# Mixer B of a two-layer hybrid encoder: when the k scaling, the weight units, the y loads and some evictions stand in the queues

## The chip, the cores and the metric

The kernel runs on one core of a Trainium2 chip. A core has five engines that run their own instruction queues in order: TensorE (PE: matmuls and transposes), VectorE (DVE), ScalarE (ACT), GpSimd (POOL) and SyncE (SP, which here only issues transfers). They meet through semaphores. Transfers run beside them. The metric is the device time of one execution in microseconds (us), the median of several runs, less is better.

## The reference

An encoder trunk of two layers over 1024 tokens of width 1024, in float32. Each layer is: RMS norm, one projection to q, k, v and a gate, attention, `(attention * silu(gate)) @ w_out`, residual; then an input embedding of 256 columns is projected, gated by a sigmoid of the normalised stream and added. Layer 0 attends over a neighbourhood (mixer A). Layer 1 (mixer B) is grouped-query attention, 16 query heads and 4 key/value heads of 64, cut to what matters here:

```python
proj = h @ w_in
q, k, v, gate = jnp.split(proj, [MIX_WIDTH, MIX_WIDTH + kv_w, MIX_WIDTH + 2 * kv_w], axis=-1)
q = rms_norm(q.reshape(b, s, B_Q_HEADS, HEAD_DIM), q_norm_g)   # per head
k = rms_norm(k.reshape(b, s, B_KV_HEADS, HEAD_DIM), k_norm_g)
q, k = _apply_axial_rope(q, tabs), _apply_axial_rope(k, tabs)
sc = einsum('bkgqd,bksd->bkgqs', q, k) / 8 ; pr = softmax(sc)
o = einsum('bkgqs,bksd->bkgqd', pr, v)
return (o * jax.nn.silu(gate)) @ w_out
```

## The kernel before

**Split operands.** Nearly every product is made from a high and a low half of each operand: `split3` issues three matmuls for one product. The stream h stands transposed in `HTh` and `HTl` (8 token tiles x 8 column blocks), weights come as units of 128 x 1024 numbers.

**Weight units.** The class `Weights` (object `WQ`) walks a fixed list of units. A unit goes through three steps: SP loads it into one of two `wstage` buffers, ACT copies it to its high half (line 235, `wh`, or `KA` where it takes such a slot), DVE subtracts to get the low half (line 240, `wl` or `KB`). Only after the subtraction is its `wstage` buffer free for the next load. `pump` does one step of this at each pulse: a unit is split when it is at least `age` pulses old, and a load is issued when at least `lag` pulses have gone by since the last split. Both are 3 in the stretch of the change. A pulse is the end of one item of the hand-written order (a piece of projection, a softmax, a block of transposes). At a pulse, actions that were put off by so many pulses (`post.add(n, f)`) also become due.

**Entry of mixer B** (about 725 to 775 us). Items in the order of `pre`: `first` (q, k, v of kv heads 0 and 1, two items to a token tile), the gate of pair 0 (`gates(0)`, two halves: matmuls `d<-HTh,KA` and `o<-HTh,KA`), then `second` (q, k, v of kv heads 2 and 3, one unit to an item, four items to a tile), with two key stacks `k_stack(0, hf)` between. `k_stack` transposes the scaled k tiles on PE (line 1277), ACT copies them (1280, 1285), POOL copies them across (1291, 1292). Each k tile is scaled by its norm in `finish_norm`: after 4 tiles DVE makes 1/sqrt in eleven small steps (lines 1206, 335 to 343), then ACT scales k (line 1236, eight 128 x 64 pieces) and POOL scales q. A gate half that is done is copied from PSUM by ACT (line 625, `G`), then goes through tanh (626). There is one PSUM buffer `d`: the next product in it waits for that copy.

**Attention steps** (from about 770 us). 128 steps n = (head, half, t). Step n puts, in this order of items: the transposes of n (`f_T`: 8 on PE into two `t` buffers, each copied by ACT to `PTh`, line 1397, and subtracted by DVE to `PTl`, line 1398), the exponentials of n + 1 (`f_E`, ACT, line 1383), the scores of n + 2 (`f_S`, PE, then DVE's minimum `mn`, line 1377), and at even n the products with V of the two steps before (`f_AV`). Projections fill the room between. A projection tile of `second` that ends there is evicted by ACT: copy to `th` (1314), square (1196), two copies to V (1320).

**The last steps.** From n = 111 or so the projection work is `pp_items`: the input embedding times its weight, copied by ACT to `th` (line 656) and stored by SP to `ppD` (line 657). `th` has two buffers, so such a copy waits until the store from two copies before has landed; the copy of a query stack (line 1349) takes a `th` buffer too. The attention result y of pairs 0 to 6 went to DRAM (`yD1h`, `yD1l`, SP, line 606) and comes back into `HTh`, `HTl` for the output projection: `load_y(1, t)`, line 290, two transfers of 448 KB for a tile. For token tiles 0 to 3 ACT's queue issues them, for 4 to 7 SP's; one tile to a step, tile t at n = 118 + t. Pair 7 stays on the chip: ACT writes its high half into `HTh` (`hi`, line 591), DVE its low half (`lo`, line 594), 3 and 5 pulses after the pair's first half is done.

The lines that the change touches, quoted where they act:

```python
                post.add(3, hi)
                post.add(5, lo)
...
                    for raw, rs in tiles:
                        post.add(2, lambda raw=raw, rs=rs: scale_tile(raw, rs, act if rs.shape[1] == 2 else pool))
...
                    if YLOAD_B <= n < YLOAD_B + NT:
                        att.append((lambda t=n - YLOAD_B: load_y(1, t), 0.0))
```

Of the kernel before, what the change touches and what calls it, by code (L numbers as in the profile page):

```python
# [15 lines left out]
AF = mybir.ActivationFunctionType  # L16
# [5 lines left out]
NT = 8  # L22
# [25 lines left out]
QO = (4, 6)  # L48
AGE, LAG = 3, 3
YS = (11, 11)  # L50
YLOAD_A, YLOAD_B = 0, 118
OPEN3 = 5
ULOAD = 5
TAGS_A = [("th", 512, 2), ("tb", 640, 2), None, ("G", 512, 3)]
# [109 lines left out]
def trunk(ctx, tc, x, wts, rpb, gains, hgains, mask, sides, rope, gain0, out):  # L164
# [196 lines left out]
    def pulse():  # L361
        WQ.pump()
        post.tick()
# [153 lines left out]
    def head_end(sb, h, hf, rs, Ops, ylive, layer, gg, talloc):  # L517
# [63 lines left out]
        def fin_last():  # L581
            dve.tensor_tensor(Y, Y, G, ALU.mult)
            if "rb" not in tail:
                post.l = [e for e in post.l if e[1] is not across]
                across()
            dve.tensor_tensor(Y, Y, tail["rb"], ALU.mult)
            y3 = Y.rearrange("p (t c) -> p t c", t=4)
            ts = slice(4 * hf, 4 * hf + 4)

            def hi():  # L590
                act.activation(HTh[:, ts, 7, :], y3, AF.Copy)

            def lo():
                dve.tensor_tensor(HTl[:, ts, 7, :], y3, HTh[:, ts, 7, :], ALU.subtract)
            if hf == 0:
                post.add(3, hi)
                post.add(5, lo)
            else:
                hi()
                lo()  # L600
# [533 lines left out]
    def mixer_b(pend):  # L1134
        with ExitStack() as es:
# [63 lines left out]
            def normed(t):  # L1199
                return range(t - 3, t + 1) if t % 4 == 3 else ()  # L1200

            def finish_norm(ss, tiles):
                wk = sb.tile([128, 96], F32, name="wk", bufs=1)
                n = ss.shape[1]
                if pro[0]:
                    ops = [lambda: dve.tensor_scalar(ss, ss, 0.5 / HD, 0.5 * EPS, op0=ALU.mult, op1=ALU.add)]
                    ops += rsqrt_ops(ss, ss, wk)
                    for i in range(2):
                        post.add(1 + i, lambda i=i: [f() for f in ops[6 * i:6 * i + 6]])
                    for raw, rs in tiles:  # L1210
                        post.add(2, lambda raw=raw, rs=rs: scale_tile(raw, rs, act if rs.shape[1] == 2 else pool))
                    return
                y, a = wk[:, 0:n], wk[:, n:2 * n]

                def power():
                    dve.tensor_scalar(ss, ss, 4.0 / HD, 4.0 * EPS, op0=ALU.mult, op1=ALU.add)
                    for c in range(0, n, 8):
                        w = slice(c, min(c + 8, n))
                        pool.tensor_tensor(y[:, w], ss[:, w], mhalf[:, :w.stop - c], ALU.pow)

                def newton():
                    dve.tensor_tensor(a, y, y, ALU.mult)
                    dve.scalar_tensor_tensor(a, a, -1.0, ss, op0=ALU.mult, op1=ALU.mult)
                    dve.scalar_tensor_tensor(ss, a, 3.0, y, op0=ALU.add, op1=ALU.mult)
                post.add(DR, power)
                at = DR + NP + (8 if n > 16 else 0)
                post.add(at - 1, newton)
                for i, (raw, rs) in enumerate(tiles):
                    post.add(at + i, lambda raw=raw, rs=rs: scale_tile(raw, rs))
# [67 lines left out]
            def qkv_items(i, eng, kstep):  # L1297
                keys = [("bqkv", i, u) for u in range(4)]
                items = []
                st = {}  # L1300
                for t in range(NT):
                    def evac(ps, t=t):
                        if t == 0:
                            KR[i] = qtp.tile([128, NT, 128], F32, name="qt")
                            for j in range(2):
                                V[2 * i + j] = vp.tile([128, NT, 128], F32R, name="V")
                            st["ss"] = sb.tile([128, NT, 6], F32, name="ss")
                        if t % 4 == 0:
                            QT[i, t // 4] = qtp.tile([128, 4, 256], F32, name="qt")
                        ss = st["ss"]  # L1310
                        tabq, tabk = st.pop("tab")
                        qt, kr = QT[i, t // 4][:, t % 4], KR[i][:, t]
                        raw = sb.tile([128, 512], F32, name="th")
                        act.activation(raw, ps, AF.Copy)
                        red = sumsq(raw[:, :384], 6, ss[:, t])
                        vs = []
                        for j in range(2):
                            v = V[2 * i + j][:, t]
                            c = raw[:, 384 + 64 * j:448 + 64 * j]
                            act.activation(v[:, :64], c, AF.Copy)  # L1320
                            vs.append((v, c))

                        def rot():
                            red()
                            rope_in(kr, raw[:, 256:384], tabk, eng)
                            rope_in(qt, raw[:, :256], tabq, eng)
                            for v, c in vs:
                                eng.tensor_tensor(v[:, 64:], c, v[:, :64], ALU.subtract)
                        post.add(1 if pro[0] else DR, rot)
                        us = normed(t)  # L1330
                        if us:
                            finish_norm(ss[:, us[0]:t + 1].rearrange("p t c -> p (t c)"),
                                        [(KR[i][:, u], ss[:, u, 4:6]) for u in us] +
                                        [(QT[i, u // 4][:, u % 4], ss[:, u, 0:4]) for u in us])

                    def alloc(t=t):
                        st["tab"] = load_tab(0, t), load_tab(1, t)
                        return dalloc()
                    items += proj_N(keys, t, 512, alloc, evac, release=keys if t == NT - 1 else (), kstep=kstep)
                return items  # L1340

# [80 lines left out]
            def gates(p):  # L1422
                return [i for hf in range(2) for i in gate_items("bg", p, hf, dalloc, sb, gg)]

            def stacks(i):
                return [(lambda hf=hf: k_stack(i, hf), 450.0) for hf in range(2)]
            first, second = qkv_items(0, dve, 4), qkv_items(1, pool, 2)
            ks, gf = stacks(0), gates(0)
            pre = first[:12] + ks[:1] + first[12:14] + [glue(lambda: q_stack(0, 0))] + first[14:]
            pre += gf + second[:2] + ks[1:] + second[2:6]  # L1430
# [2 lines left out]
            for i, d in enumerate(pre):  # L1433
                if pend and (i == 1 or i >= 2 and i % 2 == 0):
                    to_ht(psT, *pend.pop(0))
                if not pend:
                    WQ.hold = ("ple", 1, 0, 0)
                d[0]()
                pulse()
            pro[0] = False  # L1440

            def exps(n):
# [10 lines left out]
            for g in range(4):  # L1453
                att = []
                for n in range(32 * g, 32 * g + 32):
                    h, hf, t = steps[n]
                    av = n >= 2 and n % 2 == 0
                    w = CB if av else CN
                    def turn():
                        if WQ.gate:  # L1460
                            WQ.gate = False
                        later.tick()
                    att.append((turn, w[0]))
                    if av:
                        att.append((lambda n=n: f_AV(*steps[n - 1]), w[1]))
                    te = [(blocks(n), w[2])]
                    if n + 1 < len(steps):
                        te.append((exps(n + 1), w[3]))
                    if n % 2 == 0 and n > 0:
                        te.reverse()  # L1470
                    att += te
                    if n + 2 < len(steps):
                        def scores(n=n):
                            f_S(*steps[n + 2])
                            WQ.gate = n % 2 == 1 and n % 8 != 5 if n < 126 else None
                        att.append((scores, w[4]))
                    if n in (37, 41):
                        att.append((lambda n=n: turned.append(lambda: k_stack(1, n // 41)), 0.0))
                    m = n + QS_AT
                    if m % 8 == 0 and m < len(steps):  # L1480
                        hn, fn, _ = steps[m]
                        att.append((lambda hn=hn, fn=fn: turned.append(lambda: q_stack(hn // 2, fn)), 0.0))
                    if YLOAD_B <= n < YLOAD_B + NT:
                        att.append((lambda t=n - YLOAD_B: load_y(1, t), 0.0))
                if g == 3:
                    def last():
                        end[0] = 1
# [484 lines left out]
```

## Time and profile before

| | us |
|---|---|
| median of 3 runs | 1490.86 (1490.63 to 1491.48) |
| the profiled execution, its own time | 1492.02 |
| its span, first to last instruction | 1490.2 |
| around the span | 1.8 |
| PE busy in the span | 1470.3 (99%) |
| granted TensorE clock, mean | 0.999 |

In a timeline row stand the start and the length in us, the engine, the line, the operation, what it writes and reads, the sizes, how many instructions the row merges, and in brackets the engine's idle time before it with what ended it. The chain of waits is followed back from the last instruction: start, length, and what ran. A matmul's end is modelled, so matmuls overlap in the rows; two that follow each other without a wait start some 0.23 us apart, while each lasts 0.39.

### The profile page before, as it was taken

How to read it: one execution, taken by the hardware profiler on the slowest of the kernel's cores; microseconds unless marked ns; L12 is line 12 of the kernel's file. 1: busy time of each engine (PE TensorE's matmuls, PEld its weight loads, DVE VectorE, ACT ScalarE, POOL GpSimd, SP SyncE). 2: the span in 40 equal slices, each digit the busy share in tenths (PEclk: the TensorE clock that was granted, in tenths of full speed). 3: DMA queues.
4: the chain of work that ended last, by engine and by line, in shares of the span. 5: the costliest groups of instructions: out<-in, count | busy, mean ns of one | idle time of the engine just before them, and what ended most of it. 6: DMA issues, size and time to landing. Idle time of an engine off the chain costs nothing.

```text
span 1490.2 us, 23430 instructions
## 1 busy us (share of the span) xinstructions
PE 1470.3 (99%) x8305; PEld 1270.7 (85%) x8305; DVE 1053.9 (71%) x1915; ACT 914.6 (61%) x1836; POOL 464.8 (31%) x647
## 2 busy tenths in 40 slices
PE   8999999999999999999999999999999999999997
PEld 6888888988988887888878888999999988888886
DVE  5467776477477598657757687877878787689845
ACT  5477766477477635433456777777767777744532
POOL 2246775387265200020144342324141400000000
PEclk9999999999999999999999999999999999999999
DMA  8224564283122862262220111101102112763223
GB/s 262 99 89 159 103 164 138 65 170 100 36 89 85 326 254 99 92 204 86 68 78 12 40 50 45 42 17 50 51 28 64 37 64 73 246 234 109 78 95 128
DMA packets 91460, 157.61 MB, mean 106 GB/s; under 512 B 18256, under 2 KB 54352, under 8 KB 90832
## 3 DMA queue, kind: packets, MB, share of 16 engines
q1 hardware_dynamic: 87344, 143.80, 28.8%
q0 software_dynamic: 2560, 8.39, 3.8%
q10 hardware_dynamic: 1440, 3.94, 0.9%
q8 instruction: 66, 1.08, 0.3%
q14 instruction: 50, 0.41, 0.1%
HBM read 125.56 MB, written 50.83 MB: 118 GB/s over the span
## 4 chain that ended last, share of the span: by engine, by line
PE 55%; DVE 4%; ACT 2%; issue 1%; DMA 1%; POOL 0%; ACTq 0%; POOLq 0%; DVEq 0%
PE d L324 27%; PE s L324 10%; PE o L324 8%; PE t L1395 7%; PE t L506 1%; PE t L324 1%; PE t L1347 0%; DVE PTl L1398 0%; DMA HTl<-yD1l 0%; DVE xn L1749 0%; ACT wh L235 0%; DVE X L1638 0%; DVE wl L240 0%; DVE mn L1377 0%; DVE wl L1536 0%
## 5 line engine op out<-in xcount | busy, mean ns | idle before, releaser
L324 PE MATMUL d<-wh,HTh 128*128 128x512 f32 (+1 forms) x800 | 285.5, 358 | 2.0 <-ACT G L625 0.8
L324 PE MATMUL d<-wl,HTh 128*128 128x512 f32 (+1 forms) x800 | 281.7, 354 | 0.8 <-DVE wl L240 0.8
L324 PE MATMUL d<-wh,HTl 128*128 128x512 f32 (+1 forms) x800 | 282.5, 355 | 0.0
L1398 DVE TENSOR_TENSOR PTl<-t,PTh 128x512 fp32r<-128x512 f32 x256 | 164.7, 685 | 110.0 <-ACT PTh L1397 109.4
L324 PE MATMUL d<-HTh,wh 128*128 128x512 f32 x480 | 193.8, 404 | 0.0
L324 PE MATMUL d<-HTh,wl 128*128 128x512 f32 x480 | 188.7, 393 | 0.0
L324 PE MATMUL d<-HTl,wh 128*128 128x512 f32 x480 | 188.2, 392 | 0.0
L324 PEld LDWEIGHTS d<-wh,HTh 128*128 128x128 f32 x800 | 150.5, 189 | 24.8 <-ACT G L625 1.2
L324 PEld LDWEIGHTS d<-wl,HTh 128*128 128x128 f32 x800 | 150.8, 189 | 23.3 <-DVE wl L240 1.6
L324 PEld LDWEIGHTS d<-wh,HTl 128*128 128x128 f32 x800 | 150.8, 189 | 22.0 <-DVE wki L902 0.3
L1383 ACT ACTIVATE P<-s,mn 128x1024 f32<-128x1024 f32 x128 | 142.9, 1117 | 41.7 <-DVE mn L1377 40.6
L1397 ACT ACTIVATE PTh<-t 128x512 fp32r<-128x512 f32 x256 | 138.7, 594 | 42.1 <-PE t L1395 41.2
L1377 DVE TENSOR_REDUCE mn<-s 128x1 f32<-128x1024 f32 x128 | 154.8, 1210 | 5.1 <-PE s L324 4.7
L849 POOL TENSOR_TENSOR PTh<-PTh,SIDE 128x256 fp32r<-128x256 f32 x96 | 83.9, 874 | 168.2 <-ACT PTh L844 168.1
L1395 PE MATMUL t<-ident,P 128*128 128x128 f32 x1024 | 133.8, 273 | 1.3 <-DVE PTl L1398 1.3
L324 PE MATMUL s<-KA,QS 128*128 128x512 f32 (+2 forms) x384 | 134.8, 405 | 0.0
L1395 PEld LDWEIGHTS t<-ident,P 128*128 128x128 f32 x1024 | 116.6, 141 | 11.7 <-DVE PTl L1398 4.4
L324 PE MATMUL s<-KB,QS 128*128 128x512 f32 (+2 forms) x384 | 121.4, 370 | 0.0
L324 PE MATMUL o<-PTh,V 128*128 128x256 f32 (+2 forms) x672 | 118.6, 287 | 2.6 <-ACT PTh L1397 0.9
L324 PE MATMUL o<-PTl,V 128*128 128x256 f32 (+2 forms) x672 | 120.2, 290 | 0.5 <-DVE mn L821 0.5
L240 DVE TENSOR_TENSOR wl<-wstage,wh 128x1024 fp32r<-128x1024 f32 x76 | 95.0, 1252 | 34.6 <-ACT wh L235 34.5
L324 PEld LDWEIGHTS o<-PTh,V 128*128 128x128 f32 x672 | 98.6, 190 | 11.4 <-ACT PTh L1397 4.1
(286 smaller groups left out, 2930.0 us busy)
## 6 DMA issues: line engine op xcount, KB each, us to landing
wstage<-in_wts SPq DMA_DIRECT2D x88, 512.0 KB
pp<-ppD SPq DMA_DIRECT2D x32, 256.0 KB
X<-in_x SPq DMA_DIRECT2D x15, 512.0 KB
rb<-rD SPq DMA_DIRECT2D x58, 128.0 KB
ppD<-th SPq DMA_DIRECT2D x20, 256.0 KB
tD0t<-in_wts SPq DMA_DIRECT2D x16, 256.0 KB
tD1t<-in_wts SPq DMA_DIRECT2D x16, 256.0 KB
xD<-X SPq DMA_DIRECT2D x8, 512.0 KB
```

The costliest lines, as they stand in the source:

```text
L240: eng.tensor_tensor(lo[:, c:c + n], s[:, c:c + n], hi[:, c:c + n], ALU.subtract)
L324: pe.matmul(ps, a, b, start=first, stop=last, skip_group_check=True)
L506: pe.transpose(ps[:, k], xn[:, (4 * c + k) * 128:(4 * c + k + 1) * 128], ident)
L849: pool.tensor_tensor(pt[:, 3 * j - 1:3 * j + 4:4], pt[:, f1:f1 + 1].to_broadcast([128, 2, 128]), SIDE[:, :2], ALU.mult)
L1377: dve.tensor_reduce(mn, ps, axis=AX.X, op=ALU.min)
L1383: act.activation(p, ps, AF.Exp, bias=mn, scale=-1.0, accum_out=RS[h, hf][:, t:t + 1])
L1395: pe.transpose(ps[:, i], p[:, k * 128:(k + 1) * 128], ident)
L1397: act.activation(PTh[:, ks, c], ps, AF.Copy)
L1398: dve.tensor_tensor(PTl[:, ks, c], ps, PTh[:, ks, c], ALU.subtract)
```

## The change

It has five parts.

1. `KS_LATE = 5`: in the entry, the ACT scaling of k for tiles 4 to 7 is due 5 pulses after their last tile's eviction, and no longer 2. The scaling of q on POOL and of tiles 0 to 3 stays.
2. From item 14 of `pre` to its end, `WQ.age, WQ.lag` are 2, 1 where they were 3, 3.
3. `YLOAD_B = (114, 118)`: y tiles 0 to 3 are loaded at n = 114 to 117 where it was 118 to 121. Tiles 4 to 7 stay at n = 122 to 125.
4. The square and the two copies to V of an eviction of `second` are put off by one pulse once the entry is over.
5. The low half of pair 7's first half is due after 10 pulses where it was 5.

```diff
-YLOAD_A, YLOAD_B = 0, 118
+YLOAD_A, YLOAD_B = 0, (114, 118)
+KS_LATE = 5
...
-                post.add(5, lo)
+                post.add(10, lo)
...
-            def finish_norm(ss, tiles):
+            def finish_norm(ss, tiles, late=2):
...
-                        post.add(2, lambda raw=raw, rs=rs: scale_tile(raw, rs, act if rs.shape[1] == 2 else pool))
+                        key = rs.shape[1] == 2
+                        post.add(late if key else 2, lambda raw=raw, rs=rs, key=key: scale_tile(raw, rs, act if key else pool))
...
-                        red = sumsq(raw[:, :384], 6, ss[:, t])
-                        vs = []
-                        for j in range(2):
-                            v = V[2 * i + j][:, t]
-                            c = raw[:, 384 + 64 * j:448 + 64 * j]
-                            act.activation(v[:, :64], c, AF.Copy)
-                            vs.append((v, c))
+                        vs = [(V[2 * i + j][:, t], raw[:, 384 + 64 * j:448 + 64 * j]) for j in range(2)]
+                        reds = []
+
+                        def square():
+                            reds.append(sumsq(raw[:, :384], 6, ss[:, t]))
+                            for v, c in vs:
+                                act.activation(v[:, :64], c, AF.Copy)
+                        if pro[0]:
+                            square()
+                        else:
+                            post.add(1, square)
...
+                                        2 if t < 4 else KS_LATE)
...
+            age, lag = WQ.age, WQ.lag
...
+                if i == 14:
+                    WQ.age, WQ.lag = 2, 1
                 d[0]()
                 pulse()
+            WQ.age, WQ.lag = age, lag
...
-                    if YLOAD_B <= n < YLOAD_B + NT:
-                        att.append((lambda t=n - YLOAD_B: load_y(1, t), 0.0))
+                    for t in range(NT):
+                        if n == YLOAD_B[t // 4] + t:
+                            att.append((lambda t=t: load_y(1, t), 0.0))
```

The instructions of PE and POOL stand in the same order as before. ACT's, DVE's and SP's move at the places below. (Line numbers of the changed kernel are one to twelve higher.)

**ACT at the entry**, from the last eviction of `first` on. `wh` is the high half of a weight unit (the number tells units apart), `G` the copy of a gate half out of PSUM, `qt` here the k tiles that are scaled. Before:

```order
L1320 ACTIVATE V<-th 128x64 x2
L1236 ACTIVATE qt<-qt,ss 128x64 x8
L235 ACTIVATE wh_7849<-wstage 128x1024
L625 ACTIVATE G<-d 128x512
L626 ACTIVATE th<-G 128x512
L235 ACTIVATE wh_7879<-wstage 128x1024
L625 ACTIVATE G<-o 128x512
L626 ACTIVATE th<-G 128x512
L235 ACTIVATE wh_7907<-wstage 128x1024
```

Now:

```order
L1323 ACTIVATE V<-th 128x64 x2
L236 ACTIVATE wh_7799<-wstage 128x1024
L236 ACTIVATE wh_7847<-wstage 128x1024
L236 ACTIVATE wh_7859<-wstage 128x1024
L626 ACTIVATE G<-d 128x512
L627 ACTIVATE th<-G 128x512
L1238 ACTIVATE qt<-qt,ss 128x64 x8
L626 ACTIVATE G<-o 128x512
L627 ACTIVATE th<-G 128x512
```

The three units stand ahead of the k scaling, and all three now stand ahead of the first gate copy too. The load of the third (`wh_7859`) goes into the buffer that the subtraction `wl_7800` frees, which stands on DVE in the middle of the 1/sqrt steps (`wk`):

```order
L343 TENSOR_TENSOR wk<-wk,ss 128x24
L344 SCALAR_TENSOR_TENSOR wk<-wk 128x24
L342 TENSOR_TENSOR wk<-wk 128x24
L241 TENSOR_TENSOR wl_7800<-wstage,wh_7799 128x1024
L343 TENSOR_TENSOR wk<-wk,ss 128x24
L344 SCALAR_TENSOR_TENSOR wk<-wk 128x24
```

Before, no subtraction stood between these steps.

**ACT at an eviction in the attention** (steps 0 to 2). Before:

```order
L1314 ACTIVATE th<-d 128x512
L1196 ACTIVATE t_8107<-th 128x384
L1320 ACTIVATE V<-th 128x64 x2
L1397 ACTIVATE PTh<-t 128x4x128 x2
L1383 ACTIVATE P,rs<-s,mn 128x1024 x2
```

Now:

```order
L1316 ACTIVATE th<-d 128x512
L1404 ACTIVATE PTh<-t 128x4x128 x2
L1197 ACTIVATE t_8121<-th 128x384
L1323 ACTIVATE V<-th 128x64 x2
L1390 ACTIVATE P,rs<-s,mn 128x1024 x2
```

The copies to `PTh` passed the square and the V copies. This happens at three of the evictions.

**ACT at n = 114 and 115.** Before, no transfer of y stood here; now, with `L1356` the copy of a query stack into `th` (line 1349 before):

```order
L657 ACTIVATE th<-d 128x512
L1404 ACTIVATE PTh<-t 128x4x128 x2
L291 DMA HTh<-yD1h 128x896
L291 DMA HTl<-yD1l 128x896
L657 ACTIVATE th<-d 128x512
L1404 ACTIVATE PTh<-t 128x4x128 x2
L1390 ACTIVATE P,rs<-s,mn 128x1024
L291 DMA HTh<-yD1h 128x896
L291 DMA HTl<-yD1l 128x896
L1356 ACTIVATE th<-t 128x512
```

Two tiles of y are issued ahead of that copy; before, the first stood some 14 rows behind it.

More of the change, by code (lines that the diff above doesn't have):

```diff
@@ L1314, in evac @@
                         act.activation(raw, ps, AF.Copy)
-                        red = sumsq(raw[:, :384], 6, ss[:, t])
-                        vs = []
-                        for j in range(2):
-                            v = V[2 * i + j][:, t]
-                            c = raw[:, 384 + 64 * j:448 + 64 * j]
-                            act.activation(v[:, :64], c, AF.Copy)
-                            vs.append((v, c))
+                        vs = [(V[2 * i + j][:, t], raw[:, 384 + 64 * j:448 + 64 * j]) for j in range(2)]
[8 more added lines that the diff above has]
+                            post.add(1, square)
                         def rot():
-                            red()
+                            reds[0]()
                             rope_in(kr, raw[:, 256:384], tabk, eng)
@@ L1333, in evac @@
                                         [(KR[i][:, u], ss[:, u, 4:6]) for u in us] +
-                                        [(QT[i, u // 4][:, u % 4], ss[:, u, 0:4]) for u in us])
+                                        [(QT[i, u // 4][:, u % 4], ss[:, u, 0:4]) for u in us],
+                                        2 if t < 4 else KS_LATE)
                     def alloc(t=t):
```

## The prediction

> **What bounds the kernel now.** First the page:
>
> ```profile
> span 1490.2 us, 23430 instructions
> PE 1470.3 (99%) x8305; PEld 1270.7 (85%) x8305; DVE 1053.9 (71%) x1915; ACT 914.6 (61%) x1836; POOL 464.8 (31%) x647
> ```
>
> PE is busy nearly throughout, and the change neither adds nor drops a matmul, nor moves one. So it can act only through PE's waits. Second, therefore, the list of PE's waits by releaser (in total, times, longest), whose rows all fall into the stretches that the change touches or near them:
>
> ```profile
> PE o L324 <- ACT PTh L1397: 0.9, 3, 0.4
> PE d L324 <- ACT G L625: 0.8, 1, 0.8
> PE d L324 <- DVE wl L240: 0.8, 1, 0.8
> ```
>
> Third, these waits in PE's timeline, at the entry of mixer B (first three rows), at two evictions and a transpose behind them (next four), and at the end of mixer B (last three):
>
> ```profile
> 751.75 0.50 PE L324 MATMUL d<-wh,HTh 128*128 128x512 f32 x1 [0.78 <-ACT G L625]
> 756.80 0.51 PE L324 MATMUL d<-wh,HTh 128*128 128x512 f32 x1 [0.19 <-ACT wh L235]
> 758.07 0.50 PE L324 MATMUL d<-wl,HTh 128*128 128x512 f32 x1 [0.75 <-DVE wl L240]
> ...
> 775.17 0.63 PE L324 MATMUL s<-KB,QS 128*128 128x512 f32 x2
> 776.08 1.23 PE L324 MATMUL o<-PTh,V 128*128 128x256 f32 x8 [0.28 <-ACT PTh L1397]
> 793.62 1.23 PE L324 MATMUL o<-PTh,V 128*128 128x256 f32 x8 [0.28 <-ACT PTh L1397]
> 800.62 1.25 PE L1395 MATMUL t<-ident,P 128*128 128x128 f32 x8 [0.27 <-DVE PTl L1398]
> ...
> 1284.84 0.50 PE L324 MATMUL d<-wh,KA 128*128 128x512 f32 x1 [0.45 <-ACT th L656]
> 1287.15 1.25 PE L1395 MATMUL t<-ident,P 128*128 128x128 f32 x8 [0.65 <-DVE PTl L1398]
> 1298.13 1.19 PE L324 MATMUL o<-PTh,V 128*128 128x256 f32 x8 [0.54 <-DVE Y L529]
> ```
>
> The bracket understates a wait, since it counts from the modelled end of the matmul before. From the start of the pair at 775.17, two matmuls at 0.23 end their turn at 775.63; the next starts at 776.08, so 0.45 is lost where the bracket says 0.28. The first matmul behind a wait then takes some 0.1 longer. So I count each wait as its bracket plus 0.27, and only 0.17 where the next matmul waits again. Together: entry 1.05 + 0.36 + 1.13 = 2.5 us (the third starts 1.04 late, having no matmul in between, plus 0.1); evictions 0.55 + 0.55, transpose 0.54; end of mixer B 0.72 + 0.92 + 0.81 = 2.45. That is 6.6 us in all, the most that the change could bring.
>
> Fourth, the chain of waits through the entry, which says why PE waited there:
>
> ```profile
> 746.94 0.19 DVE wk L341
> ...
> 748.25 2.03 ACT qt L1236 x8
> 750.27 0.96 ACT wh L235
> 751.25 1.24 DVE wl L240
> 752.51 3.16 DMA wstage<-in_wts
> 755.69 1.07 ACT wh L235
> 756.78 1.24 DVE wl L240
> ...
> 759.47 2.72 PE o L324 x12
> ```
>
> The k scaling waits for the end of the 1/sqrt steps and holds a weight copy back for 2.03 us; its subtraction then releases a buffer late, the load takes 3.16, and copy and subtraction come late for PE's last unit. (Twelve matmuls in 2.72 us are the 0.23 used here.)
>
> **Entry: parts 1 and 2.** The copy of the gate half stands here on ACT:
>
> ```profile
> 751.13 0.57 ACT L625 ACTIVATE G<-d 128x512 f32<-128x512 f32 x1
> 751.73 0.63 ACT L626 ACTIVATE th<-G 128x512 f32<-128x512 f32 x1
> ```
>
> The waits at 756.80 and 758.07 go: the three units stand ahead of the scaling. But the gate copy now stands behind the third of them, which needs a load, and that load needs the buffer freed by the subtraction in the middle of the 1/sqrt steps. Step by step: the sixth of the eleven steps starts at 746.94, so the subtraction starts near 747.1 and ends 1.24 later, 748.35; SP issues; the load takes 3.16, so 751.53; the weight copy holds ACT for 0.96, so the gate copy starts at 752.5 and ends at 753.1, where it ended at 751.70 before. PE was through with the product ahead at 750.8, so its first wait grows from 0.94 to 2.35, or 2.45 with the restart. Behind it nothing more is late: the first two units are ready (the second's subtraction follows the 1/sqrt steps and ends near 750.6), twelve matmuls take PE to 756.0, and the k stack's transposes need the scaling, which runs behind the gate's tanh from 753.75 to 755.8. That cover is 0.2 us thin. The third unit's subtraction, as I number it here, ends near 753.9 and is wanted at 757.8. The DVE steps pushed back by 1.24 delay, beside the k scaling, only POOL's scaling of q, whose first use is a query stack of the attention.
> So 2.5 of waiting are replaced by 2.45: **-0.1**. Bounds: -2.5 if the load were there in time, +0.4 if it takes a fifth longer.
>
> **Evictions: part 4.** ACT before the wait at 776.08:
>
> ```profile
> 774.73 0.52 ACT L1196 ACTIVATE t<-th 128x384 f32<-128x384 f32 x1
> 775.16 0.39 ACT L1320 ACTIVATE V<-th 128x64 fp32r<-128x64 f32 x2
> 775.45 1.06 ACT L1397 ACTIVATE PTh<-t 128x512 fp32r<-128x512 f32 x2
> ```
>
> With square and V copies behind, `PTh` starts 0.7 earlier, more than the 0.45 that PE loses: -0.55, and the same at 793.62. The square is still read in time: DVE turns to it only after both `PTl`, which themselves follow the two `PTh`. At 800.62 PE follows a chain over DVE (`PTl`, query split, sum, minimum, exponential, copy) that starts some 0.75 earlier while PE comes 0.55 earlier; of 0.54 I take 0.3, the middle between nothing and all. Sum **-1.4**, from -0.8 to -1.7. At the third eviction that changes no wait over 0.1 stands in the list, and I count nothing.
>
> **End of mixer B: parts 3 and 5.** Two of the three waits there come from the y loads on ACT's queue, by this row of the chain and the ones behind it in the timeline:
>
> ```profile
> 1277.99 5.73 DMA HTl<-yD1l
> ```
>
> ACT cannot issue the last of the eight transfers until this one has landed, and PE's 1284.84 and 1287.15 wait for ACT. With the loads four steps earlier no y transfer is left on ACT then: -0.72 - 0.92. The third wait is for DVE's join `Y`, behind part 5's subtraction; that passes to behind the next minimum, into a DVE gap:
>
> ```profile
> 1296.71 0.68 DVE L594 TENSOR_TENSOR HTl<-Y,HTh 128x512 fp32r<-128x512 f32 x1
> ```
>
> 0.68 of 0.70 late, so -0.75. Together **-2.4**.
>
> What the loads meet four steps earlier: the store that frees the `th` buffer of the query-stack copy.
>
> ```profile
> 1251.10 1.08 ACT L1397 ACTIVATE PTh<-t 128x512 fp32r<-128x512 f32 x2
> ...
> 1251.78 0.53 SPq L216 DMA_DIRECT2D wstage<-in_wts  x1
> 1252.41 0.37 SPq L657 DMA_DIRECT2D ppD<-th  x1
> ...
> 1257.07 0.60 ACT L1349 ACTIVATE th<-t 128x512 f32<-128x512 f32 x1 [0.64 <-DMA ppD<-th]
> 1257.65 0.93 PE L1395 MATMUL t<-ident,P 128*128 128x128 f32 x7
> ...
> 1251.00:1252.00 1.00, 1.00 (x8) 0.87 (x7) 0.28 (x1) 1.00 (x3) 0.00 (x0) 1.00 0.07 25
> 1252.00:1257.00 5.00, 5.00 (x35) 4.50 (x34) 4.27 (x6) 2.85 (x6) 1.30 (x1) 1.00 0.85 256
> 1269.00:1284.00 15.00, 15.00 (x100) 13.48 (x97) 10.64 (x15) 9.39 (x16) 0.00 (x0) 1.00 0.87 273
> 1272.00:1273.00 1.00, 1.00 (x9) 0.93 (x8) 0.84 (x1) 0.49 (x1) 0.00 (x0) 1.00 1.00 400
> 1278.00:1280.00 2.00, 2.00 (x12) 1.70 (x11) 1.73 (x4) 1.66 (x4) 0.00 (x0) 1.00 0.72 159
> ```
>
> (The last five rows are stretches; their last two columns are the share of the 16 DMA engines and GB/s.) That store already lands late, 4.6 us after its issue, and ACT waits 0.64 for it. Tile 0 of y, two transfers of 448 KB, is issued at the dispatch of the `PTh` copies, from 1251.2, ahead of the store at 1252.41: 917 kB more in front of it. At the best slice, 400 GB/s, they take 2.3 us; at the mean of the y loads, 273, 3.4; at the slowest, 159, 5.8. Of the 5 us in which the store waited, 15% were free: 0.75. I take the middle of 2.3 and 3.4 less 0.75, 2.1 us. PE needs the buffer that this copy empties for the second four transposes, near 1258.1, and the copy ends at 1257.67: 0.4 to spare. So PE waits 1.7 anew. Queued behind the copy on ACT are an exponential and two `PTh`, 2.1 later too, which PE wants 2 us after and later. The store of the next `pp` copy but one stands behind tile 2 in the same way, with some 4 us until its buffer is wanted: +0.3, estimated. **+2.0**, bounds 0 and 5.4 + 0.9.
> [...]
>
> **Sum.** -0.1 - 1.4 - 2.4 + 2.0 = -1.9 us against the profiled execution's 1492.02 (span 1490.2 and 1.8 around it), so 1490.1. It lay 1.16 above the median of the runs; from the median 1490.86 it is **1489.0**. What a measurement of this kernel can tell from no change is 0.2%, 3.0 us.
>
> **Rivals.**
> - *The y loads find room.* The queue's free share and the 0.4 to spare take them in, and the +2.0 is 0 to 0.5: 1487.0 to 1487.5. For it: in the microsecond in which the new loads are issued the queues ran at 25 GB/s only. Against: the stretches above, where y and a store together kept the engines 87% busy. At nothing, -3.9, 1487.0.
> - *The gate copy isn't held.* If the third unit's load lands before ACT would come to the gate copy, the entry gives 2.5: 1486.6. For it: only that the subtraction might run earlier on DVE; it would need 2 us, and the steps before it are a chain.
> - *Slower: the store is starved.* At the slowest stretch's 159 GB/s the query-stack copy is 5.8 late, PE waits 5.4, and the later stores add 0.9: -0.1 - 1.4 - 2.4 + 6.3 = +2.4, 1493.3. The time passes that of before when the new waits exceed 3.9 us. For it: in the row of 5.73 above one y transfer took that long with two others in flight. Against: that rate held for 2 us only.
> - *Nothing arrives.* What evictions and end give is lost at the next wait (PE's `PTl` waits at 800.62 and 1287.15 follow DVE, 71% busy over the span): 1490.9.
>
> **How the numbers follow.** Forecast 0.54, within 1487.9 to 1490.5. Room for the loads 0.20, gate copy not held 0.05, starved 0.09, nothing 0.12. Faster by over 0.2% (below 1487.9): the first two rivals, with a part of the forecast's lower edge, 0.28. Slower by over 0.2% (above 1493.8): a part of the starved case, 0.05. Within: 0.67. The range for 8 in 10 reaches into the first two rivals and a third of the way to the starved one, and a little below the second of the rivals, since it can meet the first: 1486.0 to 1492.0.
>
> **What would show it.** Entry: a PE wait for `G` near 751 of about 2.2 in brackets, ACT idle before the third unit for its load, and no wait for `wh` or `wl` at 757; without the long `G` wait the entry step is wrong. Evictions: no wait for `PTh` near 776 and 793. End: the query-stack copy waiting 2 us and more for `ppD`, and a PE transpose near 1258 waiting for it; none of it, and the loads found room. No wait for `th`, `PTl` or `Y` at 1284 to 1298; if these stay, the moves didn't do what they say.

## The result, and the profile after

The changed kernel takes 1492.70 us where the kernel before took 1490.96 beside it (medians of 20 runs each): ratio 1.0013, 95% interval 1.0007 to 1.0019. It is 1.7 us slower, where 1.9 faster was forecast, and 0.7 us above the range. The profiled execution took 1493.02. Its page and PE's longest waits by releaser (in total, times, longest):

```profile
span 1491.2 us, 23440 instructions
PE 1471.2 (99%) x8305; PEld 1273.2 (85%) x8305; DVE 1052.6 (71%) x1915; ACT 913.7 (61%) x1836; POOL 465.1 (31%) x647
```

```profile
PE t L1402 <- ACT th L1356: 2.7, 1, 2.7
PE d L325 <- ACT G L626: 2.1, 1, 2.1
PE t L1402 <- DVE PTl L1405: 1.5, 2, 1.1
```

The three waits of the entry, the two for `PTh`, and those for `th` and `Y` behind 1284 are gone from the list. In their place stand the query-stack copy's, the gate copy's and one for `PTl`. Where they lie, in PE's timeline:

```profile
752.65 0.50 PE L325 MATMUL d<-wh,HTh 128*128 128x512 f32 x1 [2.11 <-ACT G L626]
...
1258.33 0.66 PE L1402 MATMUL t<-ident,P 128*128 128x128 f32 x4 [2.71 <-ACT th L1356]
...
1272.23 1.25 PE L1402 MATMUL t<-ident,P 128*128 128x128 f32 x8 [1.09 <-DVE PTl L1405]
```

PE's instructions stand in one order in every kernel here, so the time from one given matmul to another can be compared between traces. Cut at the matmuls that start at 745, 765, 810, 880, 1250, 1262, 1278 and 1309.3 in the trace of before, each trace gives its difference to before, worked out from the starts of PE's instructions (for e9 without the 14 matmuls that it adds). The stretches 880 to 1250 and behind 1309 differ by less than 0.1 in all and are left out; the stretch ahead of 745, which no edit touches, differs by -2.1 to +1.3 us from execution to execution. One profiled execution stands behind each row. (e1 to e12 are the experiments below.)

| us against before | 745-765 entry | 765-810 | 810-880 | 1250-1262 | 1262-1278 | 1278-1309 |
|---|---|---|---|---|---|---|
| after | -0.18 | -1.52 | -0.48 | +4.51 | +1.50 | -2.35 |
| e1 part 3 alone | +0.15 | +0.01 | -0.01 | +4.50 | +0.92 | -1.75 |
| e10 the same again | +0.04 | +0.02 | -0.01 | +6.00 | +0.01 | -1.75 |
| e9 part 3, wait filled | +0.07 | +0.01 | -0.01 | +2.48 | +2.74 | -1.75 |
| e12 one y transfer | +0.01 | +0.02 | 0.00 | +1.47 | 0.00 | -0.15 |
| e2 without part 3 | +1.50 | -1.52 | -0.48 | 0.00 | 0.00 | -0.39 |
| e3 parts 1, 2 | -0.19 | -0.04 | -0.01 | 0.00 | 0.00 | -0.43 |
| e4 part 1 | -2.49 | -0.04 | -0.01 | 0.00 | 0.00 | -0.83 |
| e5 parts 1, 4, 5 | -2.59 | -1.53 | -0.48 | +0.06 | -0.02 | -1.36 |
| e6 the same, y at 115 | -2.59 | -1.53 | -0.48 | +1.27 | +1.05 | -2.36 |
| e7 the same, y at 116 | -2.51 | -1.53 | -0.48 | +0.06 | +1.17 | -2.36 |

For the change: -0.18 - 1.52 - 0.48 - 2.35 = -4.5 against +6.0 where the y loads now stand. The last column needs care: e3 and e4, which edit nothing there, come out at -0.43 and -0.83, since the wait at 1284.84 was longer in the profiled execution of before than in theirs. Of these 6.0 the waits behind the copy and for `PTl` are 2.87 and 1.36 from start to start. Most of the rest is something that no row of before showed. The stretches of 3.4 us around the first wait (PE's busy time, then the other engines', the granted clock, the DMA share, GB/s):

```profile
1256.17:1259.58 3.41, 1.25 (x8) 1.13 (x9) 0.00 (x0) 1.90 (x4) 0.00 (x0) 1.00 0.91 362
1259.58:1262.99 3.41, 3.41 (x11) 2.65 (x10) 1.69 (x4) 3.09 (x6) 0.00 (x0) 0.50 0.28 67
1262.99:1266.41 3.42, 3.42 (x22) 2.99 (x21) 3.36 (x5) 2.29 (x4) 0.00 (x0) 1.00 0.80 280
```

Behind the wait the granted clock is 0.50 for 3.41 us, and PE's matmuls start some 0.43 apart in place of 0.23.

The store in front of the copy, by the chain of waits, and the next store that ACT waits for, by the timeline of ACT:

```profile
1249.73 7.84 DMA ppD<-th
...
1267.04 0.60 ACT L657 ACTIVATE th<-d 128x512 f32<-128x512 f32 x1 [1.38 <-DMA ppD<-th]
1267.42 1.77 ACTq L291 DMA_DIRECT2D HTl<-yD1l  x1
```

The first store takes 7.84 us where it took 4.55 before. The last row is ACT's own queue issuing a y transfer: it holds ACT for 1.77 us, where the same issue in e1 takes 0.46 and in e10 0.47. The late `PTl` therefore has two causes in this execution, the store and this issue; both stand in the chain that leads to it. At the entry the chain shows the gate copy held as forecast (subtraction, load, weight copy, gate copy):

```profile
746.61 1.23 DVE wl L241
...
747.87 3.16 DMA wstage<-in_wts
...
751.06 0.02 ACT wh L236
...
752.02 0.59 ACT G L626
```

### The profile page after: what moved, and what is told of

Read it like the earlier page. It is cut to its first block, busy times and chain, and to the rows that moved or that the text cites. A ratio compares the mean times of both kernels' runs of the same rounds, so it can differ in the third digit from the quotient of the medians.

```text
span 1491.2 us, 23440 instructions
## 1 busy us (share of the span) xinstructions
PE 1471.2 (99%) x8305; PEld 1273.2 (85%) x8305; DVE 1052.6 (71%) x1915; ACT 913.7 (61%) x1836; POOL 465.1 (31%) x647
## 4 chain that ended last, share of the span: by engine, by line
PE 55%; DVE 3%; ACT 1%; DMA 1%; issue 1%; SPq 0%; ACTq 0%; POOL 0%; DVEq 0%; POOLq 0%
PE d L325 28%; PE s L325 10%; PE o L325 8%; PE t L1402 7%; PE t L507 1%; DMA ppD<-th 1%; PE t L325 1%; PE t L1354 0%; DVE xn L1761 0%; DVE PTl L1405 0%; DVE X L1650 0%; DVE wl L1548 0%; DVE wl L241 0%; DMA wstage<-in_wts 0%; ACT wh L236 0%
## 5 line engine op out<-in xcount | busy, mean ns | idle before, releaser
L241 DVE TENSOR_TENSOR wl<-wstage,wh 128x1024 fp32r<-128x1024 f32 x76 | 94.8, 1250 | 31.4 <-ACT wh L236 31.3
L325 PEld LDWEIGHTS d<-HTh,wl 128*128 128x128 f32 x480 | 90.1, 188 | 20.3
```

The lines of the kernel that those rows point to most:

```text
L241: eng.tensor_tensor(lo[:, c:c + n], s[:, c:c + n], hi[:, c:c + n], ALU.subtract)
L325: pe.matmul(ps, a, b, start=first, stop=last, skip_group_check=True)
```

## Experiments

The theories: **A**, the y loads starve the store that the query-stack copy waits for, and a long wait of PE lets the clock fall; **B**, the entry's one wait of 2.3 us makes the loss; **C**, the clock differs whatever the kernel does.

### One part at a time: e1 to e4

e1, the kernel before with part 3 alone:

```diff
-YLOAD_A, YLOAD_B = 0, 118
+YLOAD_A, YLOAD_B = 0, (114, 118)
```

> The kernel before with part 3 alone (y tiles 0 to 3 loaded four steps sooner). Theory A, the y loads starve the store and PE's long wait lets the TensorE clock fall: the changed kernel lost 2.87 us at the transpose behind the query-stack copy and 1.36 at the transpose behind PTl near 1272, and the two waits near 1285 and 1287 (1.66) go, so +2.6 from waits; PE's matmuls stand at half speed for some 3.3 us behind the long wait, +1.6, in those executions where the clock falls. So 1493.6 without and 1495.2 with the fall, mean clock 0.998 or lower in most executions, and a spread of the times of some us. Theory B, the lower clock and the loss come from the entry of mixer B (its one wait of 2.3 us): here 1490.96 - 1.66 + what the store costs, no fall of the clock, mean clock 0.999 as before. Theory C, the clock differs from run to run whatever the kernel does: the clocks spread as in the changed kernel, and no run of matmuls at half speed stands right behind a wait.

Measured: 1494.67 against 1490.55, ratio 1.0024 (1.0014 to 1.0034). Part 3 alone costs 4.1 us. The three runs at a mean clock of 0.999 have a median of 1493.1, the four at 0.996 one of 1495.7; theory A had 1493.6 without a fall and 1495.2 with one. Its chain and timeline:

```profile
1251.61 8.09 DMA ppD<-th
```

```profile
1260.45 1.12 PE L1402 MATMUL t<-ident,P 128*128 128x128 f32 x4 [2.95 <-ACT th L1356]
```

e2, the changed kernel with the y loads back:

```diff
-YLOAD_A, YLOAD_B = 0, (114, 118)
+YLOAD_A, YLOAD_B = 0, (118, 118)
```

> The changed kernel with the y loads at their old steps (parts 1, 2, 4, 5 stay). Theory A: no wait for the query-stack copy near 1258; the waits near 1285 and 1287 come back; what is left is the entry (-0.2), evictions (-1.7, with the wait near 866 that went too) and the join Y (-0.7): 1488.3, and clocks of 0.999 in nearly all executions, spread as narrow as before. Theory B (entry): the time stays between 1490 and 1492 with clocks of 0.997 to 0.998, since the gate wait of 2.3 us is still there. Theory C: clocks as in the changed kernel, 1490.

Measured: 1488.16 against 1490.55, ratio 0.9982 (0.9973 to 0.9991): the other four parts bring 2.4 us. The clocks were not all at 0.999, as A had it: their mean was 0.9980, against 0.9985 before. Of theory B one thing holds: in the profiled execution the clock fell behind the entry's wait, and the entry came out at +1.50 instead of -0.18. Its stretches:

```profile
749.84:753.26 3.42, 1.45 (x6) 1.24 (x7) 1.84 (x2) 3.02 (x7) 1.40 (x3) 1.00 0.59 153
753.26:756.67 3.41, 3.41 (x12) 2.65 (x10) 0.91 (x2) 3.13 (x8) 0.00 (x0) 0.50 0.59 192
```

e3, the kernel before with parts 1 and 2 (the whole of `KS_LATE`, and `WQ.age, WQ.lag = 2, 1`), and e4 with part 1 alone. e4 against e3:

```diff
                 if i == 14:
-                    WQ.age, WQ.lag = 2, 1
+                    WQ.age, WQ.lag = 3, 3
```

> The kernel before with parts 1 and 2 alone. Theory A: three waits (2.5 us) become one of 2.3, so 1490.7, indistinguishable from before, clock 0.999; a wait of 2.3 us is too short for the clock to fall, or does it only in a few executions. Theory B: the clock falls behind this wait, 0.998 or lower in many executions, and the time is 1.6 us above that of before, 1492.5.

> The kernel before with part 1 alone (k scaled three pulses later, weight units at their old distances). By the order of the instructions ACT now has one weight copy, the gate copy and its tanh ahead of the k scaling, and no load stands between. Theory A (it is part 2 that puts the third unit and its load ahead of the gate copy): the waits for the gate copy, wh and wl of 2.5 us shrink to 0.5 or less, and the time is 1488.8; so part 2 gives back what part 1 brings. Rival D: the k scaling is the late one now, and PE's transposes of the k stack wait for it; then 1490 to 1491, with a wait for qt or KA near 758.

Measured: e3 1491.45, ratio 1.0006 (0.9997 to 1.0015); e4 1488.62, ratio 0.9982 (0.9973 to 0.9990), both against 1490.55. e3's mean clock was 0.9983, 0.9985 before: B's loss of 1.6 in many executions isn't there. So part 1 is worth 2 us and more, and part 2 takes it back. In e4 ACT's timeline shows the gate copy ahead of the k scaling with no load between:

```profile
744.39 1.04 ACT L236 ACTIVATE wh<-wstage 128x1024 fp32r<-128x1024 f32 x1
746.89 0.60 ACT L626 ACTIVATE G<-d 128x512 f32<-128x512 f32 x1 [1.46 <-PE d L325]
747.52 0.63 ACT L627 ACTIVATE th<-G 128x512 f32<-128x512 f32 x1
749.57 2.03 ACT L1238 ACTIVATE qt<-qt,ss 128x64 f32<-128x64 f32 x8 [1.41 <-DVE ss L344]
```

The copy waits for PE, not PE for the copy. Rival D, transposes waiting for the k scaling, didn't happen.

### Other steps for the y loads: e5 to e7, and one transfer alone: e12

e5 is the changed kernel without parts 2 and 3; e6 and e7 are e5 with

```diff
-YLOAD_A, YLOAD_B = 0, (118, 118)
+YLOAD_A, YLOAD_B = 0, (115, 118)      # e7: (116, 118)
```

> The changed kernel without part 2 (weight units at their old distances) and without part 3 (y loads at their old steps): parts 1, 4 and 5 stay. Part 1 alone measured 1488.6 against 1490.55 before. If parts 4 and 5 bring what the traces say (waits near 776, 793, 800 and 866: 1.7; join Y near 1298: 0.7), this one runs at 1486.2. If what they take away comes back at the next wait (DVE or ACT late elsewhere), it stays at 1488 to 1488.6.

> As the run before, with y tiles 0 to 3 loaded at n = 115 to 118, one step later than in the change. The first pair of y transfers is then issued behind the store that the query-stack copy waits for, though still ahead of that copy on ACT. Theory A (the store starves because 917 kB of y stand ahead of it in the 16 engines): no long wait near 1258; the waits near 1285 and 1287 (1.66) still go; 1484.6, and clocks as in the kernel before. Rival E (any y load ahead of the copy on ACT's queue holds ACT, or the later stores starve as much): a wait of 2 us or more at the copy or at one of the next, and 1486 to 1488.

> As the run before with y tiles 0 to 3 at n = 116 to 119, so that no y load stands ahead of the query-stack copy. Theory A: 1484.6 as with 115, since 115 was already behind the store. Rival E: clearly below the run with 115. If the fourth tile's load still holds ACT's queue at n = 119, part of the 1.66 comes back: 1485 to 1486.2.

Measured against 1491.17: e5 1485.42, ratio 0.9966 (0.9953 to 0.9978); e6 1486.25, ratio 0.9967 (0.9955 to 0.9978); e7 1485.15, ratio 0.9966 (0.9952 to 0.9979). All three beat the kernel before, by 4.9 to 6.0 us. Parts 4 and 5 do bring what the traces said (1486.2 was expected of e5). No step for the y loads brings more that these runs could tell apart: what the end gains (1.0 by the table) is lost at the stores. In e6 the y pair was issued 2.4 us behind the store of the query-stack copy, and the store still took 6.11 us; in e7, by PE's timeline, a later wait for `PTl` remains. The rows of e6 (its chain, then PE's timeline) and of e7 (PE's timeline):

```profile
1246.66 6.11 DMA ppD<-th
```

```profile
1253.52 0.66 PE L1402 MATMUL t<-ident,P 128*128 128x128 f32 x4 [1.03 <-ACT th L1356]
```

```profile
1263.36 1.25 PE L1402 MATMUL t<-ident,P 128*128 128x128 f32 x8 [0.69 <-DVE PTl L1405]
```

So theory A's condition, "ahead of the store", was too narrow: behind a pair of transfers that was issued after it, the store landed 1.2 later than in e5 (6.11 against 4.90). Rival E's numbers came out in e6: ACT's query-stack copy waited 2.20 for the store, and 1486.25 lies in its range. Of its two reasons the rows show the later landing of the stores; in e7 no y load stands ahead of the copy, and 1.17 is still lost at 1262 to 1278.

e12 is the kernel before with one of the eight y transfers moved (`load_y` takes the halves to load as a third argument):

```diff
...
+                    if n == 114:
+                        att.append((lambda: load_y(1, 0, (0,)), 0.0))    # high half of tile 0
                     if YLOAD_B <= n < YLOAD_B + NT:
-                        att.append((lambda t=n - YLOAD_B: load_y(1, t), 0.0))
+                        att.append((lambda t=n - YLOAD_B: load_y(1, t, (0, 1) if t else (1,)), 0.0))
```

> The kernel before with a single one of the eight y transfers moved: the high half of y tile 0 is loaded at n = 114, everything else stays at its step. With all of part 3 four transfers stand beside the store that the query-stack copy waits for (two ahead of it, two behind), it lands 7.4 to 8.1 us after its issue where it took 4.55, and PE loses 2.9 to 3.1 at the transposes behind the copy. Theory A (the bytes of y share the 16 engines with the store): one transfer of 459 kB, at the 273 GB/s of the y loads, adds 1.7 less the 0.75 that were free, so the store takes about 5.5, PE waits 0.6 (1.0 late, 0.4 to spare), and the time is that of before within 1 us. Rival F (any y load on ACT's queue ahead of the copy costs as much, through the queue or the order): the store takes 7 or more and PE waits over 2.

Measured: 1492.62 against 1491.28, ratio 1.0011 (1.0001 to 1.0021). Its chain and PE's timeline:

```profile
1251.62 6.38 DMA ppD<-th
```

```profile
1258.76 0.66 PE L1397 MATMUL t<-ident,P 128*128 128x128 f32 x4 [1.24 <-ACT th L1351]
```

The store takes 1.83 longer for 459 kB, 251 GB/s, with nothing taken in by the free share; PE loses 1.41 from start to start, so 0.42 were to spare. Rival F (7 us or more, a wait over 2) isn't met, though 6.38 and 1.41 lie above theory A's 5.5 and 0.6 too; without its deduction of 0.75 theory A would have had 6.25 and 1.3. So the delay fits the bytes, but one transfer alone doesn't tell their bytes from their number. With all of part 3 the store takes 3.3 to 3.5 us longer (after, e1, e10). The delays don't add up: two transfers ahead at 251 GB/s would be 3.7 already, and two behind cost 1.2 in e6.

### Does the clock follow the waits: e8, e11, and a filled wait: e9, e10

e8 and e11 lengthen ACT's work at 24 steps of the attention, to make PE wait:

```diff
+                    for _ in range(EXTRA.get(n, 0) if b == 0 else 0):
+                        act.activation(PTh[:, ks, c], ps, AF.Copy)
                     act.activation(PTh[:, ks, c], ps, AF.Copy)
```

> The kernel before, with the ACT copy to PTh repeated 3 to 8 times ahead of the real one at 24 steps of the attention (n = 34, 37, ... 103, each length four times), so that PE waits some 0 to 5 us at 24 places 12 us apart. Theory A (a long wait of PE can let the clock fall for some 3.3 us): matmuls at half speed stand right behind waits only; behind waits under 1.5 us never, behind some of those of 2 to 3 us, and behind all of those well over 3.4. Theory C (the clock falls whatever the kernel does): half-speed stretches stand anywhere, with no relation to the waits' length.

> The kernel before, with the ACT copy to PTh repeated 5 or 6 times ahead of the real one at the same 24 steps, so that PE's waits lie near 2 us, where a window of the grid may hold more or less than 1.86 us of them. Theory A: a fall of 3413 ns after every window with more than 1.88 us of standing still and after none with less than 1.85, the windows right behind a fall left aside.

Only one execution of each was taken, 1566.75 us for e8 and 1560.33 for e11. The trace records the granted clock. In all traces here but for the last 20 us of each, it fell 21 times, to 0.50, for 3413 ns (19 times) or 6827 (twice), and within one execution all falls begin at multiples of 3413 ns from each other. So each execution was cut into windows of that grid, and PE's standing still in each was added up from the starts of its instructions, leaving out pauses of 0.2 us and less. (With the short pauses counted too, the sums rise and the edges below move by some 0.1 us.) Three windows of e8, each with the one behind it:

```profile
943.10:946.52 3.42, 0.65 (x7) 0.45 (x6) 1.04 (x2) 3.30 (x6) 0.00 (x0) 1.00 0.34 126
946.52:949.93 3.41, 3.41 (x15) 2.91 (x14) 3.35 (x7) 3.01 (x7) 2.33 (x4) 0.50 0.00 0
960.17:963.58 3.41, 1.56 (x13) 1.56 (x14) 1.58 (x4) 3.32 (x6) 3.25 (x5) 1.00 0.00 0
963.58:967.00 3.42, 3.42 (x29) 3.25 (x28) 1.66 (x3) 2.79 (x6) 1.54 (x2) 1.00 0.00 0
1185.45:1188.87 3.42, 1.25 (x10) 1.25 (x11) 1.27 (x2) 3.28 (x7) 0.00 (x0) 1.00 0.02 7
1188.87:1192.28 3.41, 3.41 (x17) 3.41 (x17) 3.28 (x5) 2.97 (x6) 0.00 (x0) 0.50 0.23 73
```

Over the 14 traces of this case: all 18 windows with 2.05 us or more of standing still were followed by a fall; of the seven with 1.87 to 2.02, three were; of the 29 with 1.35 to 1.85, one, and that was itself a window at half clock. Of the windows with less, one (0.72, in e10) was followed by half clock, and it too ran at half clock already. e11's expected edge of 1.88 was too sharp (1.89, 1.95 and 1.95 brought none), the mechanism held, and theory C falls. That the sum in a window counts, and not one wait, fits e4: there a pause of 1.90 and a second one in the same window, together 2.24, brought a fall near 315 us, in mixer A, where in e5 the same place had 2.02 and none. One such place doesn't prove it.

e10 is e1 once more; e9 is the same with PE's first four transposes at n = 116 done again 14 times more in the long wait:

```diff
-                    for i in range(4):
-                        k = 4 * b + i
-                        pe.transpose(ps[:, i], p[:, k * 128:(k + 1) * 128], ident)
+                    for i in range(4 + (again if b == 0 else 0)):     # 14 at n = 116
+                        k = 4 * b + i % 4
+                        pe.transpose(ps[:, i % 4], p[:, k * 128:(k + 1) * 128], ident)
```

> The kernel with part 3 alone, and PE's first four transposes at n = 116 done again 14 times more (into the same buffer, with the same values) ahead of the transposes that wait for the query-stack copy. The copy ends when it did; PE is busy for some 1.9 us of the wait, so it stands still for 1.0 to 1.2 instead of 2.9 to 3.1. In the traces so far the clock fell for 3413 ns, on a grid of 3413 ns that is fixed within an execution, after each window of that grid in which PE stood still for 1.876 us or more, and, with one exception right behind another fall, after none with 1.851 or less. If that is the mechanism (theory A), no fall behind this wait in any execution: mean clock as in the kernel before (0.9985 where part 3 alone had 0.9974), time 1.3 us below part 3 alone (0.76 falls of 1.7 us), so some 2.6 us above the kernel before, and a spread as narrow as before's. Theory C (the clock has nothing to do with the waits): same clocks and same time as part 3 alone.

> The kernel with part 3 alone once more, beside the run with the filled wait on the same chip: 1494.5 again, mean clock 0.9974; 1.3 us above the filled one by theory A, the same by theory C.

Measured against 1490.57: e9 1494.75, ratio 1.0031 (1.0020 to 1.0043); e10 1493.25, ratio 1.0018 (1.0009 to 1.0027), 1.4 below e1's time. Half of the expectation held. With the wait filled the clock stayed up: 0.999 in six of seven runs, mean 0.9987 as in the kernel before, against 0.9981 in e10 and 0.9974 in e1. But no time came back. e9's timeline shows where it went:

```profile
1259.39 0.66 PE L1404 MATMUL t<-ident,P 128*128 128x128 f32 x4 [0.71 <-ACT th L1357]
...
1269.76 0.50 PE L326 MATMUL d<-wh,KA 128*128 128x512 f32 x1 [1.44 <-ACT th L658]
1272.98 1.25 PE L1404 MATMUL t<-ident,P 128*128 128x128 f32 x8 [0.62 <-DVE PTl L1407]
```

In this execution PE, no longer slowed, comes to the next `th` copy sooner and waits there for the next store. From 1250 to 1278 e9 loses 5.2, e1 with one fall 5.4, e10 with a fall of double length 6.0. By these three traces the stores set most of this stretch and the fall little.

All runs, taken by their mean clocks, say otherwise. At a mean clock of 0.999, e10's five runs have a median of 1493.1 and e9's six one of 1494.7. (Every trace ends with 2.4 to 5.3 us at half clock, so a mean of 0.999 leaves no room for another fall.) So with no fall on either side the kernel with the filled wait is some 1.6 slower, and no run shows why. And within one kernel the time follows the clock, by 2.6 us between 0.996 and 0.999 in e1. So in e9 the filled wait kept the clock up (0.999 in six of seven runs); what the fall behind the copy costs in the end stays open.

## Why the prediction failed, by its own steps

- **Entry, -0.1**: right. The gate copy stood behind the third unit's load (1.23, 3.16 and then 0.96 in the chain, as worked out), PE waited 2.27 + 0.1, and the stretch gives -0.18. What was not foreseen is the clock: the wait is long enough to let it fall in some executions (e2: 0.50 for 3.41 us, +1.7). That part 2 was the culprit, and part 1 alone worth 2.5, was not asked.
- **Evictions, -1.4**: right, and 0.6 short: -1.52 - 0.48. At the third eviction, near 866, PE's starts show a wait that the list of brackets leaves out (0.16, and a transpose 0.11 slower behind it); it went too.
- **End of mixer B, -2.4**: right against this execution of before, -2.35. Against e4, where the wait at 1284.84 had gone without any edit there, it would be 1.5.
- **The y loads meeting the store, +2.0**: the term that failed. The mechanism was right: the copy waited for `ppD`, PE's second four transposes for the copy, with 0.4 to spare as said. The size was not: the stretch lost 6.0, close to the upper bound of 5.4 + 0.9 = 6.3. In three places:
  - The deduction of 0.75 for the free share of the queues was wrong: one y transfer delayed the store by 1.83 (e12), where its bytes less the free share would have given 0.95. And transfers issued behind the store delay it as well (e6: 6.11, where e5 has 4.90 and before 4.55). Instead of 2.1 it came 3.3 late, and PE lost 2.87 where 1.7 was forecast.
  - The later store, put at +0.3: PE lost 1.36 there. ACT waited 1.38 for the store, then 1.77 for the issue of a y transfer, which no term had, and `PTl` came late. In e1 and e10, where that issue was short, the stretch behind 1262 lost 0.92 and 0.01 (in e10 PE came to it later, behind the longer fall).
  - The clock fall behind the first wait (0.50 for 3.41 us), some 1.6 in the stretch by the author's estimate, was in no term. By e9's trace the next store's wait takes its place where it is missing; the runs by clock speak against that: the changed kernel's five runs at a mean clock of 0.999 have a median of 1491.0, about the time of before, as -4.5 + 6.0 - 1.6 would have it. This stays open.
- So -4.5 + 6.0 = +1.5 by the traces, 1.7 by the medians. That is near the time of the rival "the store is starved", forecast at 1493.3 and given 0.09, but not by its sum: it had one wait of 5.4, where 2.87 came, and it had no clock fall. That its time came close is in part luck. The argument against it, that the slowest rate "held for 2 us only", looked at the rate alone and not at what else would share the engines with the store.

## What to carry to other kernels

Before loads are moved earlier, list every store and load that lands in the next 8 us (the store met here took 7.84, 8.09 and 8.07 in the changed kernel, e1 and e10) and who waits for it, and charge the moved bytes in full at the measured shared rate (here 251 GB/s for one transfer; for two ahead it gives 3.7 where 3.3 to 3.5 came); here a y load moved onto a store cost more than all the waits that it could end. Measure the parts of a bundled change apart: parts 1, 4 and 5 together are worth 5.7 us (e5), part 2 takes 2.3 of it back at the entry (the stretches of e3 and e4), part 3 costs 2.7 to 4.1 (e10, e1). Where PE is the bound, one wait can cost more than short ones of about the same sum that lie further apart: at the entry e2's one wait of 2.3, with a granted clock of 0.50 for 3.41 us behind it, came out 1.50 above the three waits of before (2.5 in sum), where the changed kernel, with no fall there, came out 0.18 below them.

## What the hardware showed that was not expected

In the 14 traces of this case, the last 20 us of each aside, TensorE's granted clock fell 21 times, to 0.50, for 3413 ns (19 times) or 6827 (twice). Within one execution the falls lie on a grid of 3413 ns. Half clock followed a window of this grid where PE had stood still in it for 2.05 us or more (18 of 18 windows), for 1.87 to 2.02 in three of seven, and for less in two alone, both at half clock already. These are sums over a window; the shortest wait that stood alone before a fall was 2.05 (e11). One of 2.3 did it in e2, with 1.96 of it in one window, and not in e3, where the grid cut it into 0.66 and 1.60; the grid lies differently from execution to execution (e2's fall at 753.26 and the changed kernel's at 1259.58 are 148.3 steps of 3413 ns apart). The fall at the entry cost 1.7 us (e2's +1.50 against -0.18), and falls spread the times: the changed kernel ran at mean clocks from 0.996 (median 1495.0) to 0.999 (median 1491.0).
